# Griffin-style decoder layer on one core: stacked high and low rows for the recurrence's gate products, and decode attention's loads issued one step ahead

## The chip, the cores and the metric

One core of one Trainium2 chip runs the whole program. The metric is the device time of one execution in microseconds, given as the median of the runs. Five engines work beside each other, each through its own instructions in order: TensorE (PE, matmuls, with its weight loads shown as PEld), VectorE (DVE), ScalarE (ACT), GpSimd (POOL) and SyncE (SP, which here issues the DMA transfers). They wait for one another through semaphores.

## The reference, cut to what matters

One decoder layer over 1024 prompt rows and 8 decode rows (T = 1032 columns in the kernel), D_MODEL = 1024. One large projection feeds three branches. The change touches the gates of the recurrence (branch A) and the decode rows' attention into memory (branch C):

```python
def rg_lru(xc, h0, wa, ba, wx, bx, lam):
    xblk = xf.reshape(B, T, LRU_BLOCKS, LRU_BLOCK)          # 16 blocks of 64
    r = jax.nn.sigmoid(jnp.einsum('btni,nij->btnj', xblk, wa.astype(f32)).reshape(B, T, C) + ba.astype(f32))
    i = jax.nn.sigmoid(jnp.einsum('btni,nij->btnj', xblk, wx.astype(f32)).reshape(B, T, C) + bx.astype(f32))
    log_a = -LRU_C * r * jax.nn.softplus(-lam.astype(f32))
    a = jnp.exp(log_a)
    u = jnp.sqrt(-jnp.expm1(2.0 * log_a)) * (i * xf)
    ...   # h = a_t * h + u_t over time

def mem_attn(q, mk, mv):          # decode: 8 rows, 4 heads of 256, 256 memory tokens
    s = jnp.einsum('bthd,bmhd->bhtm', q, mk).astype(jnp.float32) * (XHEAD_DIM ** -0.5)
    p = jax.nn.softmax(s, axis=-1).astype(mv.dtype)
    return jnp.einsum('bhtm,bmhd->bthd', p, mv).reshape(B, T, XW)
```

## The kernel before, in words

**Precision by splitting.** Each fp32 operand of a matmul is split into a high part (a rounding copy on ACT) and a low part (a subtraction on DVE), in `split`. `mm3` then makes three matmuls of each product: high weights by high data, high weights by low data, low weights by high data.

**The projection stage** (`project`, 0 to about 605 us) goes through 30 units of two output tiles each (`UNITS`: xq, lru, gate, k, v, q), and each unit through seven steps, which is a Strassen-like scheme: step i takes a weight quarter u_i (an add on DVE for some, then a split into u_ih and u_il) and makes 24 matmuls of 258 columns into the banks ub, uc or ud. Weight quarters are prepared three steps ahead (`ahead = 3`). Banks are read by ACT (p1s, u2s, p5s at L316; zb at L1369 or L1371) and by DVE (za and zb at L318, L320, L323), and the next product into the same bank waits for that.

**Side work.** After each step `pump` advances generators in two queues: `side[0]` (the recurrence `lru` of the eight lru units and the value rows) at each step, `side[1]` (the decode attention `dec_mem` of the four heads) at every second step. A `yield` is thus a step's distance. A scheduler in the framework then sets the final order on each engine by data dependences, free buffers and its own model; the code's order is where it starts from.

**The recurrence's gates.** For each of the 8 tiles m of 128 channels, `lru` convolves (xc), and then, in thirds of 344 columns, splits xc into xch and xcl and makes two gate products into the one buffer of bank tag "o": a (with wa) and ti (with wx). A tile of 128 channels holds two blocks of 64, so the stationary weights are 128 × 128 with two 64 × 64 blocks on the diagonal and zeros beside them. Each product is three matmuls and one tanh on ACT (L742). Names: wr is the loaded weight tile, wgh and wgl its split, g a gate's bank, tr and ti the results.

**Decode attention into memory.** `dec_mem` of head h turns the eight query rows (`dec_rows`, through a small DRAM tile), loads for each decode row b the keys (dck, two buffers) and, for every second b, two query rows broadcast to all partitions (dcq, two buffers), and multiplies and sums on DVE (dcj, L804). After a softmax it does the same with the values (dcv, in the same two buffers as dck; dcpb, in those of dcq; products dcw at L828).

Of the kernel before, what the change touches and what calls it, by code (L numbers as in the profile page):

```python
# [10 lines left out]
F32 = mybir.dt.float32  # L11
F32R = mybir.dt.float32r
AF = mybir.ActivationFunctionType
# [5 lines left out]
P = 128  # L19
D = 1024  # L20
KT = D // P
TP = 1024
NB = 8
# [36 lines left out]
class Builder:  # L60
# [652 lines left out]
    def lru(self, m, xr, yr):  # L713

        nc, io, vec = self.nc, self.io, self.vec
        col = lambda base: vec[:, base + m:base + m + 1]
        stt = nc.vector.scalar_tensor_tensor
        wr = self.z.tile([P, 256], F32, tag="wlr", name=f"wlr{m}", bufs=1)
        nc.sync.dma_start(wr, io["wlru"][m])
        cw = [col(V_CW + 8 * i) for i in range(4)]  # L720
        xc = self.zt(f"xc{m}")
        nc.scalar.activation(xc, xr, AF.Identity, bias=col(V_CB), scale=cw[3])
        buf = self.scv[:, m, :, :]
        for i in (2, 1, 0):
            d = 3 - i
            stt(xc[:, d:TP], xr[:, :TP - d], cw[i], xc[:, d:TP], op0=ALU.mult, op1=ALU.add)
            stt(xc[:, TP:T], buf[:, i, :], cw[i], xc[:, TP:T], op0=ALU.mult, op1=ALU.add)
            yield
        nc.gpsimd.tensor_copy(self.pconv[:, m, :], xr[:, TP - 3:TP])
        nc.gpsimd.tensor_copy(self.scvo[:, m, 0:2, :], buf[:, 1:3, :])  # L730
        nc.gpsimd.tensor_copy(self.scvo[:, m, 2, :], xr[:, TP:T])
        wgh, wgl = (self.z.tile([P, 256], F32R, tag=f"wg{e}", name=f"wg{e}{m}", bufs=1) for e in "hl")
        self.split(wgh, wgl, wr)
        a, ti = self.zt(f"tr{m}"), self.zt(f"ti{m}")
        for c, (t0, n) in enumerate(THIRDS):
            xch, xcl = (self.z.tile([P, n], F32R, tag=f"xc{e}", name=f"xc{e}{m}_{c}", bufs=1) for e in "hl")
            self.split(xch, xcl, xc[:, t0:t0 + n])
            yield
            for j, (dst, hb) in enumerate(((a, self.hba), (ti, self.hbx))):
                ps = self.bank("o", f"g{m}_{j}_{c}")[:, :n]  # L740
                self.mm3(ps, [((wgh[:, j * P:(j + 1) * P], wgl[:, j * P:(j + 1) * P]), (xch, xcl))])
                nc.scalar.activation(dst[:, t0:t0 + n], ps, AF.Tanh, bias=hb[:, m:m + 1], scale=0.5)  # L742
                yield

        sp2, sp4n = self.sp2[:, m:m + 1], self.sp4n[:, m:m + 1]
        stt(ti, ti, 1.0, xc, op0=ALU.add, op1=ALU.mult)
        th = self.zt(f"th{m}")
        nc.scalar.activation(th, a, AF.Tanh, bias=sp2, scale=sp2)
        yield
        nc.scalar.activation(a, a, AF.Exp, bias=sp4n, scale=sp4n)  # L750
        yield
        sq = self.zt(f"sq{m}")
        nc.scalar.activation(sq, th, AF.Sqrt)
        stt(th, a, 1.0, th, op0=ALU.add, op1=ALU.mult)
# [34 lines left out]
    def dec_mem(self, h):  # L789

        nc, io, ph = self.nc, self.io, self.dp
        qr = self.dram.tile([NB, 256], F32, name=f"dcq{h}")
        self.dec_rows(self.qdc, 2 * h, qr, "c")
        sc = ph.tile([P, 2, NB], F32, tag="dsc", name=f"dcs{h}", bufs=1)
        for b in range(NB):
            if b % 2 == 0:
                qb = ph.tile([P, 512], F32, tag="dq", name=f"dcq{b}_{h}", bufs=2)
                nc.sync.dma_start(qb.rearrange("p (b d) -> p b d", b=2), qr[b:b + 2, :].partition_broadcast(P))
            kk = ph.tile([P, 512], F32, tag="dk", name=f"dck{b}_{h}", bufs=2)
            nc.sync.dma_start(kk.rearrange("p (t d) -> p t d", t=2),  # L800
                              io["cmk"][b, :, h * 256:(h + 1) * 256].rearrange("(t p) d -> p t d", p=P))
            for kt in range(2):
                junk = ph.tile([P, 256], F32, tag="dj", name=f"dcj{b}_{h}_{kt}", bufs=1)
                nc.vector.scalar_tensor_tensor(junk, kk[:, kt * 256:(kt + 1) * 256], 1.0,  # L804
                                               qb[:, (b % 2) * 256:(b % 2 + 1) * 256], op0=ALU.mult, op1=ALU.mult,
                                               accum_out=sc[:, kt, b:b + 1])
            yield
        ps = self.bank("o", f"dct{h}")
        for kt in range(2):
            nc.tensor.transpose(ps[:NB, kt * P:(kt + 1) * P], sc[:, kt, :], self.ident)  # L810
        pr = ph.tile([NB, 256], F32, tag="dp", name=f"dcp{h}", bufs=1)
        st = self.sm.tile([P, 8], F32, tag="cst", name=f"dcst{h}", bufs=4)
        nc.vector.tensor_reduce(st[:NB, 0:1], ps[:NB, :256], axis=AX.X, op=ALU.max, negate=True)
        nc.scalar.activation(pr, ps[:NB, :256], AF.Exp, bias=st[:NB, 0:1], scale=1.0, accum_out=st[:NB, 1:2])
        nc.vector.reciprocal(st[:NB, 2:3], st[:NB, 1:2])
        nc.vector.tensor_scalar_mul(pr, pr, st[:NB, 2:3])
        pd = self.dram.tile([NB, 256], F32, name=f"dcpd{h}")
        nc.sync.dma_start(pd, pr)
        for b in range(NB):
            if b % 2 == 0:  # L820
                pb = ph.tile([P, 512], F32, tag="dq", name=f"dcpb{b}_{h}", bufs=2)
                nc.sync.dma_start(pb.rearrange("p (b k) -> p b k", b=2), pd[b:b + 2, :].partition_broadcast(P))
            vv = ph.tile([P, 512], F32, tag="dk", name=f"dcv{b}_{h}", bufs=2)
            nc.sync.dma_start(vv.rearrange("p (f k) -> p f k", f=2),
                              io["cmvT"][b, h * 256:(h + 1) * 256, :].rearrange("(f p) k -> p f k", p=P))
            for f in range(2):
                junk = ph.tile([P, 256], F32, tag="dj", name=f"dcw{b}_{h}_{f}", bufs=1)
                nc.vector.scalar_tensor_tensor(junk, vv[:, f * 256:(f + 1) * 256], 1.0,  # L828
                                               pb[:, (b % 2) * 256:(b % 2 + 1) * 256], op0=ALU.mult, op1=ALU.mult,
                                               accum_out=self.cdec[:, 2 * h + f, b:b + 1])  # L830
            yield
# [579 lines left out]
def _pack(i):  # L1411
    import numpy as np

    f = {k: np.asarray(v) for k, v in i.items()}

    def mtiles(w):
        k, m = w.shape
        return w.reshape(k // P, P, m // P, P).transpose(2, 1, 0, 3).reshape(m // P, P, k)
# [7 lines left out]
    o = {}  # L1426
# [10 lines left out]
    o["wout"] = mtiles(f["w_out"][0])  # L1437
    o["wgu"] = mtiles(f["w_gate_up"][0])
    o["wdn"] = mtiles(f["w_down"][0])
    blk = np.zeros((KT, P, 256), np.float32)  # L1440
    for j, name in enumerate(("lru_wa", "lru_wx")):
        w = f[name][0].reshape(KT, 2, 64, 64)
        for e in range(2):
            blk[:, e * 64:(e + 1) * 64, j * P + e * 64:j * P + (e + 1) * 64] = w[:, e]
    o["wlru"] = blk
    snk = f["sinks"][0]
    o["vec"] = np.concatenate(
        [cols(f["b_gates"][0]), cols(f["conv_w"][0]), cols(f["conv_b"][0]), cols(f["lru_ba"][0]), cols(f["lru_bx"][0]),
# [2 lines left out]
    q, m = np.arange(P)[:, None], np.arange(256)[None, :]  # L1451
# [47 lines left out]
```

## Time and profile before

| | |
|---|---|
| median of 3 runs (lowest to highest) | 1954.06 us (1953.9 to 1954.69) |
| profiled execution: its time, its span, granted TensorE clock | 1953.1 us, 1951.3 us, 0.998 |
| busy PE / DVE / ACT / POOL over the span | 1916.3 / 1354.2 / 960.3 / 88.5 us |
| DMA | 265.14 MB, mean 136 GB/s |
| chain of work that ended last | PE 84%, ACT 5%, DMA 5%, DVE 4%, issue 1% |

How to read what follows: busy time is the time in which an engine has an instruction running; a row of a timeline gives start, duration, engine, line, operation, output<-input, size, and in brackets the idle time of that engine before it and what ended it. Rows of waits give the waiting engine with its tile and line, whom it waited for, total us, times and the longest. Rows with three numbers parted by strokes are min, median and max in ns. Rows by stage give the window, its length, and busy us with counts for PE, PEld, DVE, ACT and POOL, then granted clock, share of the DMA engines and GB/s.

### The profile page before, as it was taken

To read this page: it belongs to the slowest core of one execution; us is meant where nothing else is said; L and a number is where in the kernel's file an instruction comes from. 1 tells how busy PE (TensorE), PEld (TensorE's weight loads), DVE (VectorE), ACT (ScalarE), POOL (GpSimd) and SP (SyncE) were. 2 spreads that over 40 slices of the span, in tenths; PEclk is the share of its full clock that TensorE was granted. 3 is DMA by queue.
4 is the path that set the end of the run, shared out by engine and by line. 5 is a ranking of instruction groups with operands and counts; after the bars stand their busy time and mean duration, and the time that the engine had idled before them with its cause. 6 is when DMAs were issued, how large, how long until landed. Compare 5 with 4: busy or idle time off the path is not lost.

```text
span 1951.3 us, 37170 instructions
## 1 busy us (share of the span) xinstructions
PE 1916.3 (98%) x14293; PEld 1886.1 (97%) x14293; DVE 1354.2 (69%) x2898; ACT 960.3 (49%) x2092; POOL 88.5 (5%) x125
## 2 busy tenths in 40 slices
PE   8999999999999999999999999999999999999997
PEld 8999999999999999989999999999999999999997
DVE  8888778777766655389877457886665656734557
ACT  6556555556556545288765234644334333412224
POOL 0000012000000000012210000000000000000000
PEclk9999999999999999999999999999999999999999
DMA  5455554463233767567525242212332222523202
GB/s 212 162 188 165 182 171 154 155 236 109 88 136 116 266 227 224 154 166 214 166 69 182 88 149 77 90 66 82 113 105 99 95 95 77 180 80 117 79 15 88
DMA packets 154850, 265.14 MB, mean 136 GB/s; under 512 B 18624, under 2 KB 76816, under 8 KB 154640
## 3 DMA queue, kind: packets, MB, share of 16 engines
q1 hardware_dynamic: 154672, 262.76, 41.8%
q8 instruction: 112, 1.84, 0.4%
q14 instruction: 66, 0.54, 0.1%
HBM read 194.75 MB, written 70.03 MB: 136 GB/s over the span
## 4 chain that ended last, share of the span: by engine, by line
PE 84%; ACT 5%; DMA 5%; DVE 4%; issue 1%; SPq 0%; ACTq 0%; POOL 0%; DVEq 0%; POOLq 0%
PE ub L293 5%; PE ub L291 5%; PE ub L292 5%; PE fb L291 4%; PE fb L292 4%; PE fb L293 4%; PE d L115 3%; PE d L116 3%; PE d L114 3%; PE ud L293 2%; PE ud L292 2%; PE ud L291 2%; PE fd L291 2%; PE fd L293 2%; PE fd L292 2%; PE brs L115 2%
## 5 line engine op out<-in xcount | busy, mean ns | idle before, releaser
L580 ACT ACTIVATE bp<-bp,bst 128x257 f32<-128x257 f32 (+1 forms) x128 | 62.8, 493 | 17.5 <-DVE bst L576 17.2
L291 PE MATMUL ub<-th,u_6h 128*128 128x258 f32 x232 | 66.0, 285 | 1.0 <-DVE zb L320 1.0
L291 PE MATMUL ub<-th,u_0h 128*128 128x258 f32 x232 | 65.4, 282 | 1.0 <-ACT zb L1371 1.0
L293 PE MATMUL ub<-th,u_0l 128*128 128x258 f32 x232 | 65.8, 284 | 0.6 <-DVE u_0l L81 0.6
L293 PE MATMUL ub<-th,u_4l 128*128 128x258 f32 x232 | 65.8, 285 | 0.3 <-DVE u_4l L81 0.3
L293 PE MATMUL ub<-th,u_2l 128*128 128x258 f32 x232 | 66.0, 285 | 0.0
L293 PE MATMUL uc<-th,u_3l 128*128 128x258 f32 x232 | 65.9, 284 | 0.0
L293 PE MATMUL ud<-th,u_1l 128*128 128x258 f32 x232 | 65.9, 284 | 0.0
L293 PE MATMUL ud<-th,u_5l 128*128 128x258 f32 x232 | 65.9, 284 | 0.0
L291 PE MATMUL uc<-th,u_3h 128*128 128x258 f32 x232 | 65.7, 283 | 0.0
L291 PE MATMUL ud<-th,u_5h 128*128 128x258 f32 x232 | 65.7, 283 | 0.0
L293 PE MATMUL ub<-th,u_6l 128*128 128x258 f32 x232 | 65.7, 283 | 0.0
L291 PE MATMUL ud<-th,u_1h 128*128 128x258 f32 x232 | 65.6, 283 | 0.0
L292 PE MATMUL ub<-tl,u_0h 128*128 128x258 f32 x232 | 65.6, 283 | 0.0
L291 PE MATMUL ub<-th,u_4h 128*128 128x258 f32 x232 | 65.6, 283 | 0.0
L291 PE MATMUL ub<-th,u_2h 128*128 128x258 f32 x232 | 65.6, 283 | 0.0
L292 PE MATMUL ub<-tl,u_2h 128*128 128x258 f32 x232 | 65.4, 282 | 0.0
L292 PE MATMUL ud<-tl,u_1h 128*128 128x258 f32 x232 | 65.4, 282 | 0.0
L292 PE MATMUL uc<-tl,u_3h 128*128 128x258 f32 x232 | 65.3, 282 | 0.0
L292 PE MATMUL ub<-tl,u_4h 128*128 128x258 f32 x232 | 65.3, 282 | 0.0
L292 PE MATMUL ud<-tl,u_5h 128*128 128x258 f32 x232 | 65.3, 282 | 0.0
L292 PE MATMUL ub<-tl,u_6h 128*128 128x258 f32 x232 | 65.2, 281 | 0.0
(830 smaller groups left out, 8041.0 us busy)
## 6 DMA issues: line engine op xcount, KB each, us to landing
ur<-win SPq DMA_DIRECT2D x120, 256.0 KB, 2.9
urf<-wgu SPq DMA_DIRECT2D x80, 256.0 KB, 2.6
scr_f<-fo SPq DMA_DIRECT2D x36, 258.0 KB, 2.0
dck<-cmk SPq DMA_DIRECT2D x32, 256.0 KB, 3.1
dcv<-cmvT SPq DMA_DIRECT2D x32, 256.0 KB, 3.1
st<-scr_q SPq DMA_DIRECT2D x32, 256.0 KB, 4.4
S1L<-scr_f SPq DMA_DIRECT2D x14, 516.0 KB, 4.7
scr_g<-za SPq DMA_DIRECT2D x12, 516.0 KB
```

Of the source, the lines that this page charges most:

```text
L114: nc.tensor.matmul(ps, sh, mh, start=i == 0, stop=False)
L115: nc.tensor.matmul(ps, sh, ml, start=False, stop=False)
L116: self.last_mm = nc.tensor.matmul(ps, sl, mh, start=False, stop=closes and i == last).ins
L291: mm(sh[:, w], xh, start=opens and k == 0, stop=False)
L292: mm(sh[:, w], xl, start=False, stop=False)
L293: self.last_mm = mm(sl[:, w], xh, start=False, stop=k == 3).ins
L580: nc.scalar.activation(x, x, AF.Exp, bias=st[:, g:g + 1], scale=-1.0, accum_out=st[:, 4 + g:5 + g])
```

## The change

**Gates.** The two diagonal blocks are put apart. For a third, tile `st[0]` gets the high part of the first 64 channels in rows 0 to 63 and their low part in rows 64 to 127; `st[1]` the same for the second 64 channels with the places exchanged (high in rows 64 to 127, low in rows 0 to 63). The stationary weights of 128 rows hold the same 64 input rows twice, and 64 columns of wa beside 64 columns of wx. One matmul with wgh and one with wgl then give both gates of these 64 channels; the two banks' rows are read by two tanh of 64 rows each. The data is split by two copies and two subtractions of 64 rows. The host packs the weights accordingly; their size is the same.

**Decode loads.** `load_keys(b + 1)` is now called ahead of the products of row b, and so is `load_values(b + 1)`; the first load of each is followed by a `yield` of its own. Buffers are as many as before.

```diff
         for c, (t0, n) in enumerate(THIRDS):
-            xch, xcl = (self.z.tile([P, n], F32R, tag=f"xc{e}", name=f"xc{e}{m}_{c}", bufs=1) for e in "hl")
-            self.split(xch, xcl, xc[:, t0:t0 + n])
+            st = [self.z.tile([P, n], F32R, tag=f"xc{e}", name=f"xc{e}{m}_{c}", bufs=1) for e in range(2)]
+            for e, (own, other) in enumerate(((low, high), (high, low))):
+                src = xc[own, t0:t0 + n]
+                nc.scalar.copy(st[e][own], src)
+                nc.vector.tensor_sub(st[e][other], src, st[e][own].bitcast(F32))
             yield
-            for j, (dst, hb) in enumerate(((a, self.hba), (ti, self.hbx))):
-                ps = self.bank("o", f"g{m}_{j}_{c}")[:, :n]
-                self.mm3(ps, [((wgh[:, j * P:(j + 1) * P], wgl[:, j * P:(j + 1) * P]), (xch, xcl))])
-                nc.scalar.activation(dst[:, t0:t0 + n], ps, AF.Tanh, bias=hb[:, m:m + 1], scale=0.5)
+            for e, (own, other) in enumerate(((low, high), (high, low))):
+                ps = self.bank("o", f"g{m}_{e}_{c}")[:, :n]
+                w = slice(e * P, (e + 1) * P)
+                nc.tensor.matmul(ps, wgh[:, w], st[e], start=True, stop=False)
+                self.last_mm = nc.tensor.matmul(ps, wgl[:, w], st[e], start=False, stop=True).ins
+                for dst, hb, rows in ((a, self.hba, own), (ti, self.hbx, other)):
+                    nc.scalar.activation(dst[own, t0:t0 + n], ps[rows], AF.Tanh, bias=hb[own, m:m + 1], scale=0.5)
                 yield
...
+        qbs, kks = [], []
+        def load_keys(b):
+            if b % 2 == 0:
+                qbs.append(ph.tile([P, 512], F32, tag="dq", name=f"dcq{b}_{h}", bufs=2))
+                nc.sync.dma_start(qbs[-1].rearrange("p (b d) -> p b d", b=2), qr[b:b + 2, :].partition_broadcast(P))
+            kks.append(ph.tile([P, 512], F32, tag="dk", name=f"dck{b}_{h}", bufs=2))
+            nc.sync.dma_start(kks[b].rearrange("p (t d) -> p t d", t=2), ...)
+        load_keys(0)
+        yield
         for b in range(NB):
-            if b % 2 == 0:
-                qb = ph.tile([P, 512], F32, tag="dq", name=f"dcq{b}_{h}", bufs=2)
-                nc.sync.dma_start(qb.rearrange("p (b d) -> p b d", b=2), qr[b:b + 2, :].partition_broadcast(P))
-            kk = ph.tile([P, 512], F32, tag="dk", name=f"dck{b}_{h}", bufs=2)
-            nc.sync.dma_start(kk.rearrange("p (t d) -> p t d", t=2), ...)
+            if b + 1 < NB:
+                load_keys(b + 1)
+            qb, kk = qbs[b // 2], kks[b]
...   # load_values(b) for pbs (dcpb) and vvs (dcv): the same edit
-    blk = np.zeros((KT, P, 256), np.float32)
-    ...
-    o["wlru"] = blk
+    wa, wx = (f[name][0].reshape(KT, 2, 64, 64) for name in ("lru_wa", "lru_wx"))
+    row = np.concatenate([wa[:, 0], wx[:, 0], wx[:, 1], wa[:, 1]], axis=2)
+    o["wlru"] = np.concatenate([row, row], axis=1)
```

What the built programs hold, at three places. The number behind a tile's name is only a counter that differs between the two programs, and lines of the code are shifted (L742 before is L749 now, L804 is L820, L1369 and L1377 are L1394 and L1402).

PE at the first gate of LRU tile 1 (behind step 4 of unit 5), before and now:

```order
L293 MATMUL ub5_1_1696<-th4_1_445,u5_4l_1734 128x258
L114 MATMUL g1_0_0_1890<-xch1_0_1855,wgh1_1849 128x344
L115 MATMUL g1_0_0_1890<-xcl1_0_1856,wgh1_1849 128x344
L116 MATMUL g1_0_0_1890<-xch1_0_1855,wgl1_1850 128x344
L291 MATMUL ud5_0_1737<-th110_275,u5_5h_1771 128x258
```

```order
L293 MATMUL ub5_1_1690<-th4_1_445,u5_4l_1730 128x258
L746 MATMUL g1_0_0_1886<-xc01_0_1849,wgh1_1843 128x344
L747 MATMUL g1_0_0_1886<-xc01_0_1849,wgl1_1844 128x344
L291 MATMUL ud5_0_1733<-th110_275,u5_5h_1767 128x258
L292 MATMUL ud5_0_1733<-tl110_276,u5_5h_1767 128x258
```

Two matmuls stand where three stood, at the same place between the steps; this holds for nearly all of the 48 gates. In the whole program PE has 48 instructions fewer, DVE 24 and ACT 72 more, and behind the projection stage no engine's order differs.

ACT over the first two gates of the same tile (u6 are weight quarters of unit 6, zb5 and za5 the gate unit's results), before and now:

```order
L80 CAST u6_2h_1940<-us6_2_1938 128x512
L742 ACTIVATE tr1_1853<-g1_0_0_1890,lruc_663 128x344
L1377 ACTIVATE zb5_1863<-zb5_1863,hbg_666 128x516
L80 CAST u6_3h_1978<-ur6_01_1725 128x512
L742 ACTIVATE ti1_1854<-g1_1_0_1933,lruc_663 128x344
L1377 ACTIVATE za5_1817<-za5_1817,hbg_666 128x1032
L1369 ACTIVATE zb5_1863<-ub5_0_1681,hbg_666 128x258
L80 CAST xch1_1_1974<-xc1_1713 128x344
```

```order
L80 CAST u6_2h_1938<-us6_2_1936 128x512
L749 ACTIVATE tr1_1847<-g1_0_0_1886,lruc_659 64x344
L749 ACTIVATE ti1_1848<-g1_0_0_1886,lruc_659 64x344
L1402 ACTIVATE zb5_1859<-zb5_1859,hbg_662 128x516
L740 CAST xc01_1_1972<-xc1_1707 64x344
L80 CAST u6_3h_1984<-ur6_01_1721 128x512
L749 ACTIVATE tr1_1847<-g1_1_0_1931,lruc_659 64x344
L749 ACTIVATE ti1_1848<-g1_1_0_1931,lruc_659 64x344
L1402 ACTIVATE za5_1811<-za5_1811,hbg_662 128x1032
L1394 ACTIVATE zb5_1859<-ub5_0_1675,hbg_662 128x258
L740 CAST xc11_1_1973<-xc1_1707 64x344
```

Each gate's bank is now read by two tanh, and the first half of the next third is copied a step earlier than the whole was.

DVE where the first decode product stands (dcj0_0 is row 0 of head 0; u2_0l the low part of a weight quarter), before and now:

```order
L81 TENSOR_TENSOR u1_6l_600<-ur1_11_337,u1_6h_599 128x512
L804 SCALAR_TENSOR_TENSOR dcj0_0_0_595,dcs0_590<-dck0_0_593,dcq0_0_591 128x256
L318 TENSOR_TENSOR za1_603<-uc1_0_604,p1s1_0_476 128x258
L804 SCALAR_TENSOR_TENSOR dcj0_0_1_597,dcs0_590<-dck0_0_593,dcq0_0_591 128x256
L318 TENSOR_TENSOR za1_603<-uc1_1_618,p1s1_1_491 128x258
L81 TENSOR_TENSOR u2_0l_633<-ur2_00_493,u2_0h_632 128x512
```

```order
L81 TENSOR_TENSOR u1_6l_596<-ur1_11_337,u1_6h_595 128x512
L318 TENSOR_TENSOR za1_599<-uc1_0_600,p1s1_0_476 128x258
L318 TENSOR_TENSOR za1_599<-uc1_1_614,p1s1_1_491 128x258
L81 TENSOR_TENSOR u2_0l_629<-ur2_00_493,u2_0h_628 128x512
L320 SCALAR_TENSOR_TENSOR zb1_632<-ub1_0_463,p5s1_0_520 128x258
L320 SCALAR_TENSOR_TENSOR zb1_632<-ub1_1_478,p5s1_1_535 128x258
L672 TENSOR_SCALAR nsnk_660<-vec_65 128x16
L674 TENSOR_SCALAR hbg_662<-vec_65 128x24
L675 TENSOR_SCALAR lruc_659<-vec_65 128x8
L676 TENSOR_SCALAR lruc_659<-vec_65 128x8
L677 SCALAR_TENSOR_TENSOR lruc_659<-vec_65 128x8
L820 SCALAR_TENSOR_TENSOR dcj0_0_0_697,dcs0_590<-dck0_0_593,dcq0_0_591 128x256
```

The first decode product is moved behind u2_0l, both zb and five small constants; the later ones follow a step or more behind their old places.

More of the change, by code (lines that the diff above doesn't have):

```diff
@@ L730, in lru @@
         nc.gpsimd.tensor_copy(self.scvo[:, m, 0:2, :], buf[:, 1:3, :])
+        low, high = slice(0, 64), slice(64, 128)
         nc.gpsimd.tensor_copy(self.scvo[:, m, 2, :], xr[:, TP:T])
@@ L794, in dec_mem @@
         sc = ph.tile([P, 2, NB], F32, tag="dsc", name=f"dcs{h}", bufs=1)
-        for b in range(NB):
-            if b % 2 == 0:
-                qb = ph.tile([P, 512], F32, tag="dq", name=f"dcq{b}_{h}", bufs=2)
-                nc.sync.dma_start(qb.rearrange("p (b d) -> p b d", b=2), qr[b:b + 2, :].partition_broadcast(P))
-            kk = ph.tile([P, 512], F32, tag="dk", name=f"dck{b}_{h}", bufs=2)
-            nc.sync.dma_start(kk.rearrange("p (t d) -> p t d", t=2),
-                              io["cmk"][b, :, h * 256:(h + 1) * 256].rearrange("(t p) d -> p t d", p=P))
+        qbs, kks = [], []
[4 more added lines that the diff above has]
+            kks.append(ph.tile([P, 512], F32, tag="dk", name=f"dck{b}_{h}", bufs=2))
+            nc.sync.dma_start(kks[b].rearrange("p (t d) -> p t d", t=2),
+                              io["cmk"][b, :, h * 256:(h + 1) * 256].rearrange("(t p) d -> p t d", p=P))
+        load_keys(0)
+        yield
+        for b in range(NB):
+            if b + 1 < NB:
+                load_keys(b + 1)
+            qb, kk = qbs[b // 2], kks[b]
             for kt in range(2):
@@ L818, in dec_mem, with load_values @@
         nc.sync.dma_start(pd, pr)
-        for b in range(NB):
[L820 to L825, printed above, removed]
+        pbs, vvs = [], []
+        def load_values(b):
+            if b % 2 == 0:
+                pbs.append(ph.tile([P, 512], F32, tag="dq", name=f"dcpb{b}_{h}", bufs=2))
+                nc.sync.dma_start(pbs[-1].rearrange("p (b k) -> p b k", b=2), pd[b:b + 2, :].partition_broadcast(P))
+            vvs.append(ph.tile([P, 512], F32, tag="dk", name=f"dcv{b}_{h}", bufs=2))
+            nc.sync.dma_start(vvs[b].rearrange("p (f k) -> p f k", f=2),
+                              io["cmvT"][b, h * 256:(h + 1) * 256, :].rearrange("(f p) k -> p f k", p=P))
+        load_values(0)
+        yield
+        for b in range(NB):
+            if b + 1 < NB:
+                load_values(b + 1)
+            pb, vv = pbs[b // 2], vvs[b]
             for f in range(2):
@@ L1439, in _pack @@
     o["wdn"] = mtiles(f["w_down"][0])
-    blk = np.zeros((KT, P, 256), np.float32)
[L1441 to L1444, printed above, removed]
-    o["wlru"] = blk
+    wa, wx = (f[name][0].reshape(KT, 2, 64, 64) for name in ("lru_wa", "lru_wx"))
+    row = np.concatenate([wa[:, 0], wx[:, 0], wx[:, 1], wa[:, 1]], axis=2)
+    o["wlru"] = np.concatenate([row, row], axis=1)
     snk = f["sinks"][0]
```

## The prediction

> **What bounds the kernel now.** I read the page's first part, then busy times by stage, then the waits of TensorE (PE) inside the stage that the change touches, then single stretches of the timeline. The whole page points at PE:
>
> ```profile
> PE 1916.3 (98%) x14293; PEld 1886.1 (97%) x14293; DVE 1354.2 (69%) x2898; ACT 960.3 (49%) x2092; POOL 88.5 (5%) x125
> ```
>
> The change lies in the projection stage (0 to about 605 us). The stage view gives, for each window, its length and then the busy time of each engine with its count of instructions:
>
> ```profile
> 60.00:200.00 140.00, 138.89 (x1142) 138.15 (x1141) 121.36 (x269) 81.57 (x154) 6.33 (x10) 1.00 0.52 171
> 200.00:400.00 200.00, 197.73 (x1624) 196.78 (x1623) 161.61 (x351) 113.45 (x216) 25.62 (x15) 1.00 0.51 169
> 400.00:600.00 200.00, 199.58 (x1645) 199.07 (x1644) 146.57 (x255) 118.47 (x224) 9.29 (x11) 1.00 0.38 134
> ```
>
> From 60 to 600 us PE is idle for 540 − 536.2 = 3.8 us. VectorE (DVE) is busy 429.5 of 540 us (80%), ScalarE (ACT) 313.5 (58%). So a matmul that goes away here shortens the stage by its own time, unless DVE or ACT then comes late; and at most some 4 us of PE waits are to be won beside it. These waits by pair (total, times, longest), window 0 to 605 us:
>
> ```profile
> PE u L209 <- ACT th L80: 6.2, 1, 6.2
> PE g L115 <- DVE xcl L81: 1.3, 1, 1.3
> PE ub L291 <- ACT zb L1371: 1.0, 1, 1.0
> PE ub L291 <- DVE zb L320: 1.0, 1, 1.0
> PE ub L293 <- DVE u_0l L81: 0.6, 1, 0.6
> PE vt L395 <- DVE v L407: 0.4, 1, 0.4
> PE ub L293 <- DVE u_4l L81: 0.3, 1, 0.3
> ```
>
> The first is the start of the program, which the change leaves alone. The other six are single events, 4.6 us together.
>
> **Part 1: stacked rows for the gates.** Each of 8 × 3 thirds needs two gate banks. Before, a bank took three matmuls of 344 columns, now two, with the same two weight tiles: 48 matmuls go. What one costs is its spacing, not its shown duration of 0.32 us, since matmuls overlap. The timeline of PE (start, duration) in the second LRU unit:
>
> ```profile
> 133.51 0.32 PE L114 MATMUL g<-xch,wgh 128*128 128x344 f32 x1
> 133.67 0.32 PE L115 MATMUL g<-xcl,wgh 128*128 128x344 f32 x1
> 133.82 0.32 PE L116 MATMUL g<-xch,wgl 128*128 128x344 f32 x1
> 133.98 0.28 PE L291 MATMUL ud<-th,u_5h 128*128 128x258 f32 x1
> ```
>
> From 133.51 to 133.98 are 0.47 us for three, 0.157 us each: 48 × 0.157 = **7.5 us** off PE's own work. (The Trainium skill, "TensorE: Matmul & The Clock Gate", section on the back-to-back issue gap, gives N/2.4 + 2.5 ns for an isolated warm matmul, an estimate of 146 ns at 344 columns and 7.0 us in all; and it gives 131 ns for 512 columns in a stream with weight loads, by which 48 would be worth under 6.3 us. The rows show 157 ns in such a stream, so the trace stands against the second figure, and the measurement decides.)
>
> What is added, per third: one more copy on ACT, one more subtraction on DVE, two more tanh on ACT, all on 64 rows instead of 128. Their full-height forms now:
>
> ```profile
> L80 ACT CAST xch<-xc x24: 468/478/483, 63.1 to 578.9; 128x344 fp32r<-128x344 f32 x24
> L81 DVE TENSOR_TENSOR xcl<-xc,xch x24: 498/510/519, 66.5 to 579.5; 128x344 fp32r<-128x344 f32 x24
> L742 ACT ACTIVATE tr<-g,lruc x24: 539/548/554, 67.7 to 584.6; 128x344 f32<-128x344 f32 x24
> L742 ACT ACTIVATE ti<-g,lruc x24: 525/548/556, 70.2 to 588.0; 128x344 f32<-128x344 f32 x24
> ```
>
> Does half the height cost half? Later stages have 64-row and 128-row instructions of one width beside each other:
>
> ```profile
> L607 ACT COPY bob<-bo x64: 352/368/371, 843.0 to 1038.4; 64x256 f32<-64x256 f32 x64
> L406 ACT CAST v<-vt x8: 361/370/377, 392.3 to 414.7; 128x256 fp32r<-128x256 f32 x8
> L608 DVE TENSOR_TENSOR bob<-bo,bob x64: 402/416/419, 843.6 to 1038.8; 64x256 f32<-64x256 f32 x64
> L407 DVE TENSOR_TENSOR v<-vt,v x8: 411/418/425, 393.6 to 417.0; 128x256 fp32r<-128x256 f32 x8
> ```
>
> 368 against 370 ns, 416 against 418: height is free, so each half costs a whole. L607 also crosses from rows 64–127 to rows 0–63 at no extra duration. ACT gains 24 × (0.478 + 2 × 0.548) = 37.8 us, DVE 24 × 0.51 = 12.2 us. Over 540 us ACT goes from 58 to 65%, DVE from 80 to 82%.
>
> This work lies beside PE as long as the engines are ahead of it. They are: ACT spends the stage waiting for PE to release weight buffers, and DVE for PE's sums:
>
> ```profile
> ACT u_1h L80 <- PE uc L292: 32.2, 19, 2.2
> DVE za L318 <- PE uc L293: 14.8, 18, 1.1
> ```
>
> Where is it tight? The one bank "o" must be read by two tanh, not one, before the next gate writes it. Gates of one third are one step apart, 24 matmuls of 0.12 us plus the gate itself, so about 3.2 us; the two tanh take 2 × 0.548 = 1.1 us of it. Only in the first unit does the new order leave 16 matmuls between the starts of g0_0_0 and g0_1_0 (14 others, 2.0 us), with a copy and two tanh between them on ACT: 0.478 + 1.1 = 1.6 us plus what ACT still has in hand. I take **+0.3 us** there and another **+0.3 us** for places I cannot see; bounds: 0 (all hidden, ACT's waits above) and 24 × 0.548 = 13.2 us (in every third the second tanh lies bare on PE's path). The first subtraction depends on the same chain copy, subtract as before; the second half has a step more time, so the split itself I cost at nothing, covered by that step. If the cover is gone, it costs as xcl's 1.3 us above.
>
> **Part 2: decode loads a step ahead, with a yield behind the first load.** DVE's waits on decode transfers (window 0 to 605 us):
>
> ```profile
> DVE dcw L828 <- DMA dcv<-cmvT: 8.1, 6, 3.5
> DVE dcj L804 <- DMA dck<-cmk: 6.0, 4, 4.9
> DVE dcw L828 <- DMA dcpb<-dcpd: 4.7, 3, 2.1
> DVE dcj L804 <- DMA dcq<-dcq: 2.2, 3, 1.0
> ```
>
> 21.0 us of DVE idle time, nearly all hidden. What reaches PE is to be seen where these waits and PE's meet:
>
> ```profile
> 49.02 0.43 DVE L804 SCALAR_TENSOR_TENSOR dcj<-dck,dcq 128x256 f32<-128x256 f32 x1 [0.46 <-DMA dcq<-dcq]
> 269.75 0.69 DVE L81 TENSOR_TENSOR u_3l<-ur,u_3h 128x512 fp32r<-128x512 f32 x1
> 275.35 0.43 DVE L804 SCALAR_TENSOR_TENSOR dcj<-dck,dcq 128x256 f32<-128x256 f32 x1 [4.92 <-DMA dck<-cmk]
> 324.99 0.43 DVE L828 SCALAR_TENSOR_TENSOR dcw<-dcv,dcpb 128x256 f32<-128x256 f32 x1 [3.52 <-DMA dcv<-cmvT]
> 415.04 0.43 DVE L828 SCALAR_TENSOR_TENSOR dcw<-dcv,dcpb 128x256 f32<-128x256 f32 x1 [2.05 <-DMA dcpb<-dcpd]
> ```
>
> DVE runs in order, so a product that waits holds u_0l (0.6 us of PE at 50 us), xcl (1.3 at 276), the zb sums (1.0 at 329) and v (0.4 at 417) behind it. Two of the four waits are for the broadcast rows (dcq, dcpb); these have the new yield, two steps of slack, between load and first use, and the order on DVE shows the first product gone from ahead of u2_0l. I count both as won: 0.6 + 0.4 = **−1.0 us**. The other two are for dck and dcv. With two buffers the load of b+1 can start no earlier than when the product of b−1 is done, as before; the edit moves its place in SP's queue, not that limit. And the place of all later products shifts, so where they meet DVE's full stretches is new. Between 0 and 2.3 us I take half: **−1.15 us**. The transfers themselves are the same in number and size; on SP's queue they now stand a slot earlier or later among the weight loads, and each waits only for a DVE product of the step before. I cost that at nothing: the weight splits have their buffers three steps ahead; if SP is held, u_0l to u_6l come late next. The later products also leave more of them after 440 us, where DVE has room (146.57 of 200 us).
>
> **Sum.** −7.5 + 0.3 + 0.3 − 1.0 − 1.15 = −9.05 us. The work behind the projection stands in the same order, so it follows 1:1. On the profiled execution, 1953.1 us (span 1951.3), this makes 1944.05; the median of the runs, 1954.06, is 0.96 above it: **1945.0 us**. With all six waits gone: −7.5 − 4.6 = −12.1, 1942.0.
>
> **Rivals.** (a) *The decode edit does nothing*: the waits for dck and dcv come back elsewhere and the won 1.0 with them, since transfers were already hoisted as far as two buffers let them. −7.5 + 0.6: 1947.2; up to 1950 if 3 us more waits appear. For it: the buffer limit above; against: the yield is a true slack. Chance 0.19.
> (b) *DVE falls behind.* It has full stretches and empty ones close together:
>
> ```profile
> 160.00:180.00 20.00, 20.00 (x168) 20.00 (x168) 20.00 (x45) 13.25 (x22) 2.11 (x3) 1.00 0.65 218
> 200.00:220.00 20.00, 20.00 (x164) 20.00 (x163) 13.40 (x45) 10.33 (x22) 0.00 (x0) 1.00 0.71 225
> ```
>
> Successive DVE instructions overlap a little, as these do (0.68 us long, 0.60 apart):
>
> ```profile
> 44.41 0.68 DVE L81 TENSOR_TENSOR u_4l<-us,u_4h 128x512 fp32r<-128x512 f32 x1
> 45.01 0.68 DVE L81 TENSOR_TENSOR u_5l<-us,u_5h 128x512 fp32r<-128x512 f32 x1
> ```
>
> If a subtraction that writes other rows than it reads loses this overlap with its neighbours, four times 0.08 us per third, DVE's bill is 24 × (0.51 + 0.32) = 20 us. If half of it is paid on PE's path: −7.5 + 10 = +2.5, 1956.6, the same within what can be told. Against it: the gates of unit 2 run at 200 to 223 us, after the full stretch. Chance 0.10. (The Trainium skill, "VectorE: DVE Perf Modes", section on two Vector instructions with no wait between them, has this rule: an instruction whose start quadrant changes is held until all earlier ones are done. No row before shows such a pair.)
> (c) *ACT holds bank "o".* If the second tanh comes so late that each of the 48 gate pairs of matmuls waits 0.3 us for the bank, that is 14.4 us: −7.5 + 14.4 = +6.9, 1961.0, slower. It decides from 7.5/48 = 0.16 us per gate on; for that ACT must be 2 us behind at every gate, which its waits for PE speak against. Chance 0.08.
>
> **The numbers.** Forecast 0.63. This kernel's measurement can tell some 0.2%, 3.9 us, from no change. Faster (under 1950.2): forecast, and nearly all of (a), 0.81; within: (b) and a rest of (a), 0.11; slower: (c), 0.08. The range goes from 1941.0 (1942.0 and a little for waits too short to be listed) to 1953.0 (part of (b)).
>
> **What the changed profile would show.** 96 gate matmuls, 0.157 us apart; 64-row copies near 478, subtractions near 510, tanh near 548 ns; PE's waits up to 600 us, without the start, 2 to 4 us; no wait of u_0l near 50 us; the stage's end some 9 us earlier and all that follows at its old length. I am wrong if gate matmuls wait for ACT again and again, if the half-height instructions last longer than the whole ones, or if DVE waits for dck and dcv as long as before and PE with it.

## The result, and the profile after

| | before | after |
|---|---|---|
| median of the runs beside each other | 1953.19 us | 1948.76 us |
| ratio, 95% interval | | 0.998 [0.9973, 0.9988] |
| forecast | | 1945.0 us, −9.05 us |
| profiled execution: time, span, granted clock | 1953.1, 1951.3, 0.998 | 1948.25, 1946.5, 0.998 |

The kernel became faster by 3.9 us (0.2% of 1954; by the interval 2.3 to 5.3 us), under half of what was forecast. The first part of the page after:

```profile
PE 1909.1 (98%) x14245; PEld 1878.9 (97%) x14245; DVE 1369.1 (70%) x2922; ACT 995.7 (51%) x2164; POOL 77.6 (4%) x125
```

PE has 48 matmuls less and 7.2 us less to do; ACT has 72 instructions and 35.4 us more, DVE 24 and 14.9 us more. Two gate matmuls in PE's timeline, and the groups of the new instructions (count: min/median/max in ns), from the view of the tile xc and that of line 749:

```profile
201.39 0.32 PE L746 MATMUL g<-xc,wgh 128*128 128x344 f32 x1
201.55 0.32 PE L747 MATMUL g<-xc,wgl 128*128 128x344 f32 x1
```

```profile
L740 ACT CAST xc<-xc x48: 459/467/482, 62.1 to 576.0; 64x344 fp32r<-64x344 f32 x48
L741 DVE TENSOR_TENSOR xc<-xc,xc x48: 509/511/515, 65.3 to 576.5; 64x344 fp32r<-64x344 f32 x48
```

```profile
L749 ACT ACTIVATE tr<-g,lruc x48: 529/542/547, 67.0 to 584.0; 64x344 f32<-64x344 f32 x48
L749 ACT ACTIVATE ti<-g,lruc x48: 538/544/551, 67.6 to 584.6; 64x344 f32<-64x344 f32 x48
```

Spacing 0.16 us, and half the height at the whole price: as forecast. The stages are not (window, length, busy PE, PEld, DVE, ACT, POOL, clock, DMA share, GB/s; the last row adds the three windows):

```profile
60.00:200.00 140.00, 138.92 (x1138) 137.67 (x1137) 124.70 (x274) 91.10 (x173) 8.63 (x10) 1.00 0.52 170
200.00:400.00 200.00, 198.08 (x1633) 197.11 (x1633) 166.62 (x341) 129.14 (x249) 12.27 (x15) 1.00 0.49 163
400.00:600.00 200.00, 196.32 (x1617) 195.40 (x1617) 154.51 (x288) 129.54 (x245) 6.96 (x11) 1.00 0.43 144
sum 540.00, PE 533.31 PEld 530.18 DVE 445.84 ACT 349.78 POOL 27.86; mean PE 177.77 PEld 176.73 DVE 148.61 ACT 116.59 POOL 9.29
```

PE stood idle for 540 − 533.3 = 6.7 us of the stage, 2.9 us more than before (3.8). Its waits up to 605 us:

```profile
PE u L209 <- ACT th L80: 6.4, 1, 6.4
PE vt L395 <- DVE v L407: 2.6, 2, 1.6
PE ub L291 <- ACT zb L1396: 2.0, 4, 0.7
PE g L746 <- ACT ti L749: 1.0, 1, 1.0
PE u L209 <- ACT thw L80: 0.5, 1, 0.5
PE ub L291 <- DVE zb L320: 0.4, 1, 0.4
PE ub L293 <- DVE u_4l L81: 0.3, 1, 0.3
PE dct L826 <- ACT ti L749: 0.2, 1, 0.2
PE g L746 <- DVE xc L741: 0.2, 1, 0.2
```

Without the first row and thw (the program's start) that is 6.7 us against 4.6. The wait of u_0l near 50 us is gone, and that for the low part is 0.2 us (xc L741) for 1.3 (xcl). ACT reads the bank ub too late four times instead of once (zb L1396, 2.0 us for 1.0), ACT's ti at a gate is new, and the value rows (vt) went from 0.4 to 2.6 us. In PE's timeline the last step of the projection begins 4.1 us earlier (644.1 us for 648.3; the projection thus ends near 650 us, not at about 605), and what follows keeps its length to about 1 us.

### The profile page after: what moved, and what is told of

Its sections match the earlier page's. It is cut to its first block, busy times and chain, and to the rows that moved or that the text cites. A ratio compares the mean times of both kernels' runs of the same rounds, so it can differ in the third digit from the quotient of the medians.

```text
span 1946.5 us, 37209 instructions
## 1 busy us (share of the span) xinstructions
PE 1909.1 (98%) x14245; PEld 1878.9 (97%) x14245; DVE 1369.1 (70%) x2922; ACT 995.7 (51%) x2164; POOL 77.6 (4%) x125
## 4 chain that ended last, share of the span: by engine, by line
PE 79%; DVE 7%; DMA 5%; ACT 5%; issue 2%; SPq 0%; ACTq 0%; DVEq 0%; POOL 0%; POOLq 0%
PE fb L291 4%; PE fb L292 4%; PE fb L293 4%; PE ub L293 4%; PE ub L291 4%; PE ub L292 4%; PE d L115 3%; PE d L116 3%; PE d L114 3%; PE ud L293 2%; PE ud L292 2%; PE fd L291 2%; PE ud L291 2%; PE fd L293 2%; PE fd L292 2%
```

## The experiments

Two theories for the missing 5 us. U: the added 64-row instructions of the gates come back to PE. T: the decode edit, with its two yields per head, takes what the gates win. Every kernel below is timed against the kernel before on the same chip; a ratio of 0.001 is 1.95 us.

**Each half of the change alone.** `e1_gates_only` is the kernel before with the gates' part of the diff and the packing of the weights, `e2_decode_only` the kernel before with the decode part.

> The stacked gates alone, decode attention as it was before. Theory T (the moved decode work gives back part of the 7.5 us): 6 to 8 us below the kernel before, and no PE wait on the value rows' subtraction near 400 us. Rival U (the added copies, subtractions and tanh give it back): 3 to 5 us below, with the same PE waits on ACT's zb and on the gates' bank as in the changed kernel.

> The decode loads a step ahead alone, gates as before. Theory T: 2 to 4 us above the kernel before, with the two PE waits behind the value rows (2.6 us in the changed kernel). Rival U: 0 to 1 us below, since the waits for the broadcast rows go.

Measured: e1 0.998 [0.9971, 0.9989], 1950.67 us against 1954.11; e2 1.0002 [0.9991, 1.0012], 1954.7 us. The gates alone give what the whole change gives; the decode edit gives and takes nothing that can be told (−1.8 to +2.3 us by its interval). T, which asked for 6 to 8 us from the gates alone, falls. In e1's trace PE waits 2.4 us for ACT's zb, as U had it, but only 0.2 us at the gates' bank. What the edit does to DVE is seen after (window 0 to 605 us):

```profile
DVE dcj L820 <- DMA dck<-cmk: 4.1, 3, 2.0
DVE dcw L853 <- DMA dcv<-cmvT: 3.9, 6, 1.0
DVE dcj L820 <- issue: 2.8, 1, 2.8
DVE dcw L853 <- DMA dcpb<-dcpd: 1.4, 3, 0.7
DVE dcj L820 <- DMA dcq<-dcq: 0.4, 1, 0.4
```

12.6 us of DVE idle time for 21.0 before. It was idle time beside PE. And where a wait does reach PE, it has only moved; DVE's timeline after, at the value rows:

```profile
401.76 0.42 DVE L820 SCALAR_TENSOR_TENSOR dcj<-dck,dcq 128x256 f32<-128x256 f32 x1 [1.99 <-DMA dck<-cmk]
...
402.11 0.69 DVE L276 TENSOR_TENSOR us<-ur,ur 128x512 f32<-128x512 f32 x1
402.72 0.42 DVE L407 TENSOR_TENSOR v<-vt,v 128x256 fp32r<-128x256 f32 x1
...
408.48 0.43 DVE L820 SCALAR_TENSOR_TENSOR dcj<-dck,dcq 128x256 f32<-128x256 f32 x1 [2.80 <-issue]
...
410.70 0.42 DVE L407 TENSOR_TENSOR v<-vt,v 128x256 fp32r<-128x256 f32 x1
```

The yields put the last head's keys beside the value rows. Idle stretches of 1.99 us (for dck) and 2.80 us (the view names no releaser) hold `v` behind them, and PE waits 2.6 us for it where it waited 0.4 before. That is 2.2 us more; u_0l's wait, which went, was 0.6.

**The 48 matmuls alone.** `e3_two_products` takes the third matmul from the kernel before and adds nothing; it leaves out both mixed products (high weights by low data, low weights by high data). `e4_third_kept` is the changed kernel with a third matmul per bank, whose result the next one overwrites.

```diff
  # e3, against before
-                self.mm3(ps, [((wgh[:, j * P:(j + 1) * P], wgl[:, j * P:(j + 1) * P]), (xch, xcl))])
+                w = slice(j * P, (j + 1) * P)
+                nc.tensor.matmul(ps, wgh[:, w], xch, start=True, stop=False)
+                self.last_mm = nc.tensor.matmul(ps, wgl[:, w], xcl, start=False, stop=True).ins
  # e4, against after
+                nc.tensor.matmul(ps, wgh[:, w], st[e], start=True, stop=True)
                 nc.tensor.matmul(ps, wgh[:, w], st[e], start=True, stop=False)
```

> The kernel before with two matmuls per gate instead of three (the third product, and so some of the result's precision, is left out), with ACT's and DVE's work as before. It prices the 48 matmuls alone. Both theories: 7 to 8 us below the kernel before, if a matmul that goes shortens the stage by its own time; under 5 us if other waits fill the place. Against the gates-only kernel it is equal by T, 3 us lower by U.

> The changed kernel with 48 extra gate matmuls whose result is overwritten (the number of before), all else as in the changed kernel. If PE is the bound at these places: 7 to 8 us above the changed kernel, that is 3 us above the kernel before. If the matmuls lie beside waits: under 5 us above the changed kernel.

Measured: e3 0.9958 [0.9945, 0.9971], 1946.61 us; e4 1.0023 [1.0013, 1.0032], 1958.07 us. Without them the kernel before gains 0.0042 × 1954 = 8.2 us; with them back the changed kernel loses 0.0043 × 1954 = 8.4 us. So 48 matmuls are worth about 8 us, 0.17 us each, and what is added takes about 4 us of it: e1 against e3 is 0.0022 × 1954 = 4.3 us (1.2 to 7.4 by the two intervals).

**Which of the added instructions.** f1 and f2 start from e3 and make one part of the added work each, in its own rows; f3 is e1 with one full tanh per bank, so that two quarters of the gates are taken from the wrong weights.

```diff
  # f1_split_halves, against e3
-            self.split(xch, xcl, xc[:, t0:t0 + n])
+            for r in (slice(0, 64), slice(64, 128)):
+                self.split(xch[r], xcl[r], xc[r, t0:t0 + n])
  # f2_tanh_halves, against e3
-                nc.scalar.activation(dst[:, t0:t0 + n], ps, AF.Tanh, bias=hb[:, m:m + 1], scale=0.5)
+                for r in (slice(0, 64), slice(64, 128)):
+                    nc.scalar.activation(dst[r, t0:t0 + n], ps[r], AF.Tanh, bias=hb[r, m:m + 1], scale=0.5)
  # f3_one_tanh, against e1
-                for dst, hb, rows in ((a, self.hba, own), (ti, self.hbx, other)):
-                    nc.scalar.activation(dst[own, t0:t0 + n], ps[rows], AF.Tanh, bias=hb[own, m:m + 1], scale=0.5)
+                dst, hb = ((a, self.hba), (ti, self.hbx))[e]
+                nc.scalar.activation(dst[:, t0:t0 + n], ps, AF.Tanh, bias=hb[:, m:m + 1], scale=0.5)
```

> Two matmuls per gate as in e3_two_products (both mixed products high times low are left out), one tanh per bank, but the split of each third made by two 64-row copies and two 64-row subtractions that stay in their own rows: ACT +24 x 0.467 = 11 us, DVE +24 x 0.51 = 12 us against e3_two_products. Theory S (the split is what gives the 4 us back: DVE and ACT late before the gates): 1950 to 1951, that is 3 to 4 us above e3_two_products (0.9958 of the kernel before), about 0.998. Theory H (the halved tanh gives it back, by holding bank o and by making ACT late to read the sums in ub): 1946 to 1947.5, 0.996. Both share it: about 1948.5, 0.997.

> Two matmuls per gate as in e3_two_products (both mixed products high times low are left out), the split whole, but every tanh made as two 64-row tanh in their own rows: ACT +48 x 0.54 = 26 us, nothing on DVE. Theory S: 1946 to 1947.5, 0.996 of the kernel before. Theory H: 1950 to 1951, 0.998, with waits of PE for ACT at g or at ub (ACT zb) of some 3 us. Both share it: about 1948.5.

> Stacked split as in e1_gates_only (each 64-row subtraction writes the other rows than it reads), but one full-height tanh per bank, so that two quarters of the recurrence's gates are taken from the wrong weights: part of the computation is changed, its amount on PE and DVE is that of e1_gates_only, ACT has 48 tanh less (26 us). Against f1_split_halves it differs in the crossing alone. Theory S with a crossing that costs (subtractions held by their neighbours): f3 above f1 by 2 us or more, DVE instructions behind the subtractions 0.06 us or more further apart. Theory S without: f3 as f1, 1950 to 1951. Theory H: f3 as f1, 1946 to 1947.5.

Measured: f1 0.997 [0.9959, 0.9981], f2 0.9977 [0.9967, 0.9987], f3 0.996 [0.9948, 0.9972]. f3 has the whole stacked split (24 copies and 24 subtractions more, crossing rows) and is as fast as e3, which has none of it. The split is not told apart from nothing: 0.4 us by f3, 2.3 by f1, each with some 3 us of uncertainty. The halved tanh cost 3.7 us in f2 against e3, and 3.9 us in e1 against f3 (0.002), each just clear of that. f2 and f3 came out as theory H of these expectations has it, f1 at the value named for both causes together.

**The place or the amount.** The halved tanh could cost because a bank is held for the second one, or because ACT has 26 us more to do, wherever it stands. g1 and h2 add 64-row tanh to f3 a step behind their bank, in place on finished values, where no bank waits: one per bank in g1, three in h2 (`for r in (low, high, low)`).

```diff
  # g1_tanh_elsewhere, against f3
                 yield
+                nc.scalar.activation(dst[own, t0:t0 + n], dst[own, t0:t0 + n], AF.Tanh, scale=0.5)
```

> f3_one_tanh (stacked split, one tanh per bank, part of the computation changed) with two more 64-row tanh per third, in place on finished values, each one step behind its bank's own tanh: ACT does as much as in e1_gates_only (+48 x 0.54 = 26 us against f3_one_tanh), but no bank waits for the added ones. Theory H1 (it is the amount of ACT work: in-order ACT comes later to the sums in ub): as e1_gates_only, about 1950.5, 0.998 of the kernel before, excess gaps of PE from 60 to 605 us near 11 us. Theory H2 (it is the place: bank o is held and the gates or what follows them come late): as f3_one_tanh, about 1946.5, 0.996, excess gaps near 7 us.

> f3_one_tanh with three further 64-row tanh behind every bank's own instead of the one of g1_tanh_elsewhere, a step later and in place (part of the computation is changed): ACT +144 x 0.49 = 71 us against f3_one_tanh, three times g1's. No bank waits for them. H1 (amount): the loss grows with it, at least three times the 3.5 us between f3 and g1, 1957 or more, 1.002 and above, with PE waiting for ACT at ub many times. H2 (place): 1946.5 to 1950, since ACT still has room (58 + 13 = about 73% of the stage).

("Excess gaps" there are the starts of matmuls that come more than 0.04 us later than the usual spacing of their kind, summed from 60 to 605 us of PE's timeline: 7.2 us before, 11.4 after, 10.9 in e1, 6.6 in f3.) Measured: g1 0.9983 [0.9973, 0.9993], h2 0.9997 [0.9987, 1.0007], excess gaps 8.3 and 13.8 us. g1's time is e1's, as the theory of the amount had it; its gaps are nearer to f3's. h2 lies between the two forecasts: the loss grows with the amount, but less than in proportion to g1's. The windows' sums (60 to 600 us) of the kernels, one fence each, in the order e3, f3, f1, g1, f2, e1, h2:

```profile
sum 540.00, PE 536.20 PEld 533.54 DVE 434.96 ACT 315.66 POOL 42.00; mean PE 178.73 PEld 177.85 DVE 144.99 ACT 105.22 POOL 14.00
```

```profile
sum 540.00, PE 536.61 PEld 534.53 DVE 449.78 ACT 328.12 POOL 36.40; mean PE 178.87 PEld 178.18 DVE 149.93 ACT 109.37 POOL 12.13
```

```profile
sum 540.00, PE 536.27 PEld 533.90 DVE 447.56 ACT 328.55 POOL 36.18; mean PE 178.76 PEld 177.97 DVE 149.19 ACT 109.52 POOL 12.06
```

```profile
sum 540.00, PE 535.47 PEld 532.99 DVE 448.06 ACT 345.12 POOL 36.04; mean PE 178.49 PEld 177.66 DVE 149.35 ACT 115.04 POOL 12.01
```

```profile
sum 540.00, PE 535.02 PEld 531.02 DVE 431.17 ACT 343.89 POOL 42.31; mean PE 178.34 PEld 177.01 DVE 143.72 ACT 114.63 POOL 14.10
```

```profile
sum 540.00, PE 534.34 PEld 530.68 DVE 444.58 ACT 349.92 POOL 34.48; mean PE 178.11 PEld 176.89 DVE 148.19 ACT 116.64 POOL 11.49
```

```profile
sum 540.00, PE 531.68 PEld 527.83 DVE 440.53 ACT 383.80 POOL 40.85; mean PE 177.23 PEld 175.94 DVE 146.84 ACT 127.93 POOL 13.62
```

| kernel (48 matmuls fewer in each) | ACT busy, 60–600 us | PE idle, 60–600 us | time against before | distance from before at one clock, us (estimate) |
|---|---|---|---|---|
| e3 | 316 | 3.8 | 0.9958 | −7.2 |
| f3, f1 | 328, 329 | 3.4, 3.7 | 0.9960, 0.9970 | −6.5, −5.6 |
| f2, g1 | 344, 345 | 5.0, 4.5 | 0.9977, 0.9983 | −4.7, −4.7 |
| e1, after | 350, 350 | 5.7, 6.7 | 0.9980, 0.9980 | −3.9, not known |
| h2 | 384 | 8.3 | 0.9997 | −0.3 |

PE's idle time and the kernel's time rise with ACT's busy time and not with DVE's (f2 has DVE's least, f3 its most). From f3 to h2 the price is 0.0037 × 1954 = 7.2 us for 71 us of tanh (144 of 0.49 us; ACT's busy time, in which neighbours overlap, grows by 56 us): on average 0.10 us of time for each us of tanh.

The last column takes the granted clock out, which differs between the runs. In the traces it falls to 0.5 for 3.4 us at single places, so each costs some 1.7 us: none such in before, after, f1, f3 and h2 between their first 15 and last 30 us, one in e1 (at 706 us), two in f2 (54 and 764 us) and two in g1 (702 and 760 us), behind the projection. The first of g1's, with the clock third from the end:

```profile
702.00:705.40 3.40, 3.40 (x17) 3.40 (x18) 1.43 (x3) 1.55 (x4) 0.00 (x0) 0.50 0.72 254
```

The mean clock of each run is on record, and 0.001 of 1951 us is 1.95 us. With every run taken back to a clock of 0.998 by that, the mean times lie from before's on the same chip by the column's figures, each to ±1 or 2 us. They follow the order of ACT's busy time, and f2, where a bank waits for the halved tanh, and g1, where none does, come out alike. By the times, then, the amount counts, and that the place adds to it is not shown. The traces, one of each kernel, speak more for the place: the last matmul of the projection starts 5.4 us behind f3's in e1, 7.2 in f2 (one drop of the clock in it) and 7.3 in h2, but only 1.0 in g1. So place and amount are not parted for good.

How the amount gets to PE is less plain. The start times of the projection's steps in the traces of f3 and e1 show e1 falling behind at nine places from 70 to 355 us, by 0.3 to 0.7 us each, about 4 us in all. The two largest of PE's waits for ACT in h2, without the program's start:

```profile
PE ub L291 <- ACT zb L1380: 3.1, 4, 1.4
PE drt_c L794 <- ACT ti L749: 1.3, 1, 1.3
```

At L1380 ACT reads ub too late four times. But each time ACT had stood idle for DVE within 3 us before (1.2, 1.0, 2.0 and 2.9 us), and the first of the four, at 121 us, is the wait that the kernel before has too. Only the wait at drt_c ends a stretch of 12 us of ACT without a pause, with nine of the added tanh in it. It is the same at the four late reads of the changed kernel, with 1.0 to 2.8 us of ACT idle for DVE; one of them, in ACT's timeline and PE's:

```profile
481.59 0.21 ACT L1415 ACTIVATE qds<-za 128x8 f32<-128x8 f32 x1 [1.69 <-DVE za L323]
481.71 1.04 ACT L383 ACTIVATE hi_q<-za 128x1024 fp32r<-128x1024 f32 x1
482.65 0.37 ACT L1396 ACTIVATE zb<-ub 128x258 f32<-128x258 f32 x1
```

```profile
483.07 0.39 PE L291 MATMUL ub<-th,u_0h 128*128 128x258 f32 x1 [0.72 <-ACT zb L1396]
```

ACT was not behind with its work here: a spill that waits for DVE's sum za stands ahead of the bank's read, in order. How the added tanh make such meetings more frequent was not followed, and stays open.

**Getting the 4 us back, with the whole computation.** `f4_pool_copy` is e1 with the second copy of each third on POOL. `g2_dma_swap` has one full tanh per bank into tiles that mix both gates, and three DMAs per third that put the rows right; `h1_swap_later` is g2 with one more `yield` ahead of the recurrence.

```diff
  # f4, against e1
-                nc.scalar.copy(st[e][own], src)
+                (nc.scalar.copy, nc.gpsimd.tensor_copy)[e](st[e][own], src)
  # g2, against e1 (wx1 and wa1 change places in the packed weights, the biases are packed to match)
...   # the tiles mix[0], mix[1] and un take the place of a, ti and th
-                for dst, hb, rows in ((a, self.hba, own), (ti, self.hbx, other)):
-                    nc.scalar.activation(dst[own, t0:t0 + n], ps[rows], AF.Tanh, bias=hb[own, m:m + 1], scale=0.5)
+                hb = (self.hba, self.hbx)[e]
+                nc.scalar.activation(mix[e][:, t0:t0 + n], ps, AF.Tanh, bias=hb[:, m:m + 1], scale=0.5)
+                nc.gpsimd.dma_start(un[own, t0:t0 + n], mix[e][high, t0:t0 + n])
+                if e == 1:
+                    nc.gpsimd.dma_start(mix[0][high, t0:t0 + n], mix[1][low, t0:t0 + n])
                 yield
+        yield
+        a, ti, th = mix[0], un, mix[1]
```

> The whole computation as in e1_gates_only, but the second of the two 64-row copies of each third is made by GpSimd (POOL) instead of ACT: ACT -24 x 0.467 = 11 us, POOL +24 x its own time, which no row shows (bounds from POOL's and ACT's rows: 0.5 to 1.5 us, 12 to 36 us in all, POOL being busy 4% of the time). Theory S through ACT's lateness, or theory H (ACT late in all): 1947.5 to 1949.5, 1 to 3 us under e1_gates_only. If the subtraction behind the POOL copy comes later than before and DVE is what is late: 1950.5 to 1952.

> The whole computation, with the stacked split and two matmuls per gate bank, but one full-height tanh per bank, into a tile that holds both gates (tr's rows and ti's of one block); three DMAs per third on POOL's queue (88 KB each, 72 in all) put the rows of the two gates where the recurrence wants them, and one step more lies between the last third and the recurrence. ACT -26 us against e1_gates_only. Under H (the halved tanh give the 4 us back), and if the DMAs land within the step: as f3_one_tanh, 1946 to 1948, 0.996, 2 to 4 us under e1_gates_only. If ACT or DVE wait for the DMAs at the recurrence's start and hold what PE needs: 1950 to 1953.

> g2_dma_swap with two steps instead of one between the last third and the recurrence, so that the DMAs have landed when ACT and DVE come to their rows; the whole computation. If those waits (in g2_dma_swap ACT 9.3 us, DVE 5.7 us, on the DMA from ti's rows) were what cost it the gain: 1946 to 1949, 0.996 to 0.9975 of the kernel before, and the waits gone. If it is the new order of the side work, or the DMAs' own traffic, that costs: 1950 to 1953, 0.999 to 1.0005, whatever those waits do.

Measured: f4 1.0004 [0.9994, 1.0013], g2 1.0005 [0.9994, 1.0016], h1 1.0032 [1.0018, 1.0045]. All three are slower than e1. In f4 a copy takes POOL 0.76 us (ACT 0.47), and PE waits for DVE at ub; the first row is the tile xc's, the second one of PE's waits:

```profile
L740 POOL CAST xc<-xc x24: 469/764/1515, 63.4 to 579.1; 64x344 fp32r<-64x344 f32 x24
```

```profile
PE ub L291 <- DVE zb L320: 4.2, 2, 3.0
```

h1 still had 8.6 us of ACT waits for the swapped rows (g2: 13.8, of them 9.3 for tr and 4.5 for un), so the extra step did not take them away, and DVE waited longer for weights (2.7 us in g2):

```profile
DVE us L276 <- DMA ur<-win: 6.0, 4, 2.0
```

Which of the two, the order or the transfers, costs g2 its gain was not settled. From 60 to 600 us f4, g2 and h1 have ACT busy for 338, 316 and 315 us and PE idle for 8.6, 8.1 and 7.7 us: less on ACT than in e1, and more idle time, so ACT's amount is not the only thing that counts. A part of f4's and h1's time is the clock; at one clock, by the estimate above, they stand 2.0 us below and 1.2 us above before. No kernel with the whole computation beat the changed one.

## Why the prediction was wrong, by its own steps

**The 48 matmuls (−7.5 us): right.** 8.2 and 8.4 us by e3 and e4, 7.2 by e3 at one clock. The spacing in the timeline, 0.157 us, was the right row. The estimate from the figure for a stream in the Trainium skill ("TensorE: Matmul & The Clock Gate", section on the back-to-back issue gap), under 6.3 us in all, lies further off, though e3's interval (5.7 to 10.7 us) still holds it.

**The added work's own size (ACT +37.8, DVE +12.2 us): right.** 467, 511, 542 and 544 ns for the halves; from 60 to 600 us ACT has 36.3 us more, DVE 16.3.

**"This lies beside PE" (+0.3 and +0.3 us): the step that failed.** It measured 4.3 us (e1 against e3; 3.3 at one clock). It was not bank "o" in the first unit; PE's wait there and at all other gates is 1.2 us in sum. The lead was read from totals: ACT's long waits for PE (u_1h 32.2 us) show that ACT is ahead on average, and 65% busy sounds like room. But an engine in order is late in single spots: at the four late reads of ub an instruction of 1.04 to 1.26 us (xc, ge, a spill), held up by DVE, stands ahead of the read. The row for it was quoted: PE already waited 1.0 us for ACT's zb before. That more work on ACT brings more such losses is seen in the order of the kernels above; the steps from the one to the other are not shown. At h2's 0.10 us per us, the 37.8 us would cost 3.8 us. The bounds (0 to 13.2 us) held it; the value chosen lay at their lower end. ACT's timeline after shows a spot:

```profile
351.96 0.54 ACT L749 ACTIVATE tr<-g,lruc 64x344 f32<-64x344 f32 x1
352.39 1.05 ACT L383 ACTIVATE hi_q<-zb 128x1024 fp32r<-128x1024 f32 x1
353.47 0.55 ACT L749 ACTIVATE ti<-g,lruc 64x344 f32<-64x344 f32 x1
```

The spill's copy hi_q got between the two tanh of one bank, and this is the 1.0 us of PE's wait at g, the plainest place where the halving itself shows in PE's waits.

**Decode loads (−1.0 and −1.15 us): failed.** 0 by e2 (1.0002). u_0l's wait went, as forecast; vt's, counted as won (0.4), came back as 2.6. Rival (a) had this right, "come back elsewhere"; that the measured time also lies within its 1947.2 to 1950 is in part luck, since it too gave the added work 0.6 us. With 8.2 for 7.5, 4.3 for 0.6 and 0 for 2.15 the sum is −3.9 us: the gates alone and the decode edit alone add up to the whole change.

**Rivals (b) and (c).** (b)'s mechanism is there and costs nothing that can be told (last section; f3 is as fast as e3). (c) asked for 0.3 us at each gate; there were two waits for ti in all, 1.2 us (g and dct).

**What the profile would show.** Right: 96 gate matmuls, the durations, no u_0l near 50 us, later stages at their length. Wrong: PE's waits 6.7 us instead of 2 to 4, the projection 4.1 us earlier instead of 9. Of the three signs of being wrong none came as written: a gate waited for ACT once, no half-height instruction lasted longer than the whole one, and DVE's waits for dck and dcv fell from 14.1 to 8.0 us.

## What to carry to other kernels

Work given to an engine that runs beside the bound is not free because that engine has idle time: here it cost on average 0.10 us of the end for each us of tanh on ACT, at 58 to 71% busy, while 12 us on DVE, at 80%, cost nothing that could be told. So price such work by a rate, found by adding dummy work as in h2, before counting what is taken from the bound as won. The rate says nothing of work taken away: f4, g2 and h1 took work from ACT and lost time against e1. Differences of 2 us ask for a look at the clock of each run first. And idle time of a side engine that a better prefetch removes is worth only what of it the bound waits for, and may land in a worse place.

## What the runs showed of the hardware

Neighbours on one engine overlap, and lose it where one stands on other rows. DVE's timeline after, a pair of whole height and a pair whose first one is a subtraction of 64 rows into the other 64:

```profile
195.08 0.68 DVE L81 TENSOR_TENSOR u_0l<-ur,u_0h 128x512 fp32r<-128x512 f32 x1
195.68 0.42 DVE L820 SCALAR_TENSOR_TENSOR dcj<-dck,dcq 128x256 f32<-128x256 f32 x1
...
202.48 0.51 DVE L741 TENSOR_TENSOR xc<-xc,xc 64x344 fp32r<-64x344 f32 x1 [0.27 <-ACT xc L740]
203.02 0.69 DVE L81 TENSOR_TENSOR u_3l<-ur,u_3h 128x512 fp32r<-128x512 f32 x1
```

The first pair starts 0.60 us apart for a duration of 0.68, the second 0.54 apart for 0.51: 0.08 us of overlap became 0.03 us of gap, 0.11 us for each such neighbour. It holds throughout: behind the 32 subtractions whose next instruction had nothing to wait for, the median gap is 0.03 us, and DVE's other neighbours from 60 to 600 us overlap by a median of 0.08. This is the rule weighed in rival (b) (the Trainium skill, "VectorE: DVE Perf Modes", on two Vector instructions with no wait between them), and the trace agrees. ACT, of which that rule does not speak, does the same; its timelines before and after:

```profile
201.07 0.55 ACT L742 ACTIVATE tr<-g,lruc 128x344 f32<-128x344 f32 x1
201.52 1.15 ACT L1377 ACTIVATE za<-za,hbg 128x1032 f32<-128x1032 f32 x1
```

```profile
203.37 0.54 ACT L749 ACTIVATE tr<-g,lruc 64x344 f32<-64x344 f32 x1
203.93 0.54 ACT L749 ACTIVATE ti<-g,lruc 64x344 f32<-64x344 f32 x1
204.37 0.47 ACT L740 CAST xc<-xc 64x344 fp32r<-64x344 f32 x1
```

0.10 us of overlap before, 0.02 us of gap between tr and ti, which read different rows of the bank (over 47 such pairs the median gap is 0.01 us). It is not the height: the copy behind them, of 64 rows too, overlaps by 0.10 us again. So a half-height instruction can take from ACT about 0.1 us more than it would in a stream of whole ones.
